# Strassen–Winograd chains of the ConvFFN up-projection: the first sum's split and the second sum's transfer taken earlier in the split order

## The chip, the cores and the metric

The kernel runs on one core of a Trainium2 chip. The metric is the device time of one execution in microseconds (us), smaller is better.

## The reference, cut to what matters

The reference is a small causal decoder trunk in fp32: one attention layer and one recurrent (RG-LRU) layer on x of 512 tokens by 1024 features, each followed by a gated ConvFFN. What the change touches is the up-projection `x @ w_up` of the ConvFFN:

```python
D_MODEL = 1024
SEQ = 512
DEPTH = 2
D_FF = 3 * D_MODEL
FFN_CONV_WIDTH = 3
...
def conv_ffn(x, w_up, conv_w, conv_b, w_down):
    u = causal_dwconv(x @ w_up, conv_w, conv_b)
    g, v = u[..., :D_FF], u[..., D_FF:]
    return (jax.nn.gelu(g, approximate=True) * v) @ w_down
...
    for layer in range(DEPTH):
        ...
        x = x + rms_norm(h, norm_mix_post[layer])
        h = rms_norm(x, norm_ffn_pre[layer])
        h = conv_ffn(h, ffn_w_up[layer], ffn_conv_w[layer], ffn_conv_b[layer], ffn_w_down[layer])
        x = x + rms_norm(h, norm_ffn_post[layer])
```

`w_up` is 1024 by 6144 in each of the two layers.

## The kernel before, in words

**Splitting.** Every fp32 operand of a matmul is split into two tiles, hi (ScalarE, ACT, copies the block to the matmul's format, L211) and lo (VectorE, DVE, subtracts hi from the block, L212). A product is then three matmuls: hi·hi, hi·lo and lo·hi. One split of a 128x512 block is one ACT and one DVE instruction.

**Chunks and chains.** The up-projection of a layer is cut into 24 chunks of 256 output features, each 1 MB of weights, loaded by SyncE (SP, `load`, L408) into a `raw` tile of four blocks of 128x512. There are three `raw` buffers. Of the 24 chunks, 20 a layer (`SEVEN`: ten indices, two halves each) go through `seven`. There a chunk is a *chain*: a Strassen–Winograd step that makes the 2x2 block product with seven products of 128 features, 512 inputs and 256 tokens instead of eight. Layer 0's chains take the trace from about 530 to 790 us, layer 1's from about 1077 to 1330 us.

**The sums of weight blocks.** A chain needs sums of its four blocks. They are made in place. The blocks are called w11, w12, s1 (which arrives as A21) and a22:

- `ahead`: s1 += block a22, which gives the first sum S1. An accumulating DMA of 256 KB, issued by GpSimd (POOL, L248), which reads the block from memory again.
- `across`: s1 += block w11, the second sum S2. The same kind of DMA. It may start only when S1 has been split, since it overwrites it.
- `left`: w11 += block A21, which gives the third sum S3. The same kind of DMA, after w11 has been split.
- `lower`: w12 += s1 on DVE (L274), the fourth sum S4.

So a chain has seven splits, named by what they hold: w11, w12, s1, s2, s3, s4, a22. Product 1 reads w11, 2 reads w12, 3 reads s4, 4 reads a22, 5 reads s1, 6 reads s2 and 7 reads s3.

**What sets the order.** `stream` (L260) makes for all 20 chains of a layer one list of items (splits, and issues of transfers and adds). Each item has a position: ten per chain (`CYCLE`), plus an offset that is written down in a table. The list is sorted by position and only the resulting order counts. `pump` (L366) takes pieces off the head of the list when fewer than 14 of the split pairs are in use (`HALVES`). A split is then written to ACT's and DVE's program at that point. Each engine runs its instructions in program order, so a split that waits for a transfer holds up all that stands behind it on ACT and on DVE. A POOL issue likewise stands in POOL's program in the order of the list, and waits there for the split of the block that it overwrites.

**The other user of these engines.** TensorE (PE) runs the products in a fixed order with a few plain products filled in between (`quarters`, `rows`). Their results are taken out by ACT and DVE: `part<-ps` copies of products 1, 5 and 6 (ACT L1124), an add of `part` into the PSUM tile after product 3 (DVE L1128), another after product 7 (DVE L1133), the convolution's first tap (ACT L845) and other taps (DVE L849), GELU (ACT L867) and the gate's multiply (DVE L871). Product 4 of a chain accumulates onto what L1133 wrote, so PE waits for L1133 there. `L1115` is the matmul line of all chain products.

Of the kernel before, what the change touches and what calls it, by code (L numbers as in the profile page):

```python
# [125 lines left out]
def kernel(  # L126
# [112 lines left out]
    def blocks(i):  # L239

        raw = raws[i]
        return {
            n: raw[:, 4 * b : 4 * b + 4, :] for b, n in enumerate(("w11", "w12", "s1", "a22"))
        }

    def add_block(i, to, b):
        assert i < state["dma"]
        nc.gpsimd.dma_start(blocks(i)[to], plan[i][3][0][0][:, 4 * b : 4 * b + 4, :], accum_op=ALU.add)  # L248

    def ahead(i):  # L250
        add_block(i, "s1", 3)

    def free_slots(n):

        end = CYCLE * n
        free = [CYCLE * c + r for c in range(n) for r in ((6, 7, 9) if c < 2 or c > 13 else (6, 7))][2:] + [end, end + 1]
        assert not {CYCLE * c + a for c in range(n) for a in AT.values()} & set(free)
        return free

    def stream(i0, n):  # L260

        items = []
        for c in range(n):
            i, o = i0 + c, CYCLE * c

            def left(i=i):
                add_block(i, "w11", 2)

            def across(i=i):
                add_block(i, "s1", 0)  # L270

            def lower(i=i):
                x = blocks(i)
                nc.vector.tensor_tensor(x["w12"], x["w12"], x["s1"], op=ALU.add)  # L274

            if c:
                items.append((o - 7, (None, lambda i=i: ahead(i))))
            for at, item in (
                (-6, ("w11", "w11")), (-5.9, (None, left)), (0, ("s1", "s1")), (0.4, ("w12", "w12")),
                (1.5, (None, across)), (5, ("s2", "s1")), (5.1, (None, lower)), (7, ("s3", "w11")),  # L280
                (8.5, ("s4", "w12")), (10.6, ("a22", "a22")),
            ):
                if isinstance(item[0], str):
                    item = ((i, item[0]), lambda i=i, h=item[1]: [blocks(i)[h]], item[0] == "a22")
                items.append((o + at, item))
        free = free_slots(n)
        direct = up["direct"]
        at = 8
        for key, loads, cuts, length in direct:
            u = free[at]  # L290
            if loads:
                items.append((u - EARLY, (None, loads)))
            items.append((u - 1, ((i0, key), cuts, False)))
            at += length
        return [item for _, item in sorted(items, key=lambda x: x[0])]
# [42 lines left out]
    def refill():  # L338

        i = state["cv"]  # L340
        if i >= state["dma"]:
            return
        if plan[i][0] == "quad":
            pieces.extend(strided_stream(i))
            state["cv"] += 24
            return
        if plan[i][0] == "seven":
            n = 1
            while plan[i + n][0] == "seven":
                n += 1  # L350
            pieces.extend(stream(i, n))
            state["cv"] += n
        else:
            if plan[i + 1 : i + 2] and plan[i + 1][0] == "seven":
                pieces.append((None, lambda: ahead(i + 1)))
            parts = parts_of(plan[i][0], raws[i])
            pieces.extend(plain(i, j, r, j == len(parts) - 1) for j, r in enumerate(parts))
            state["cv"] += 1
# [1446 lines left out]
```

## Time and profile before

| what | value |
|---|---|
| median of 3 runs | 1431.22 us (1428.69 to 1431.68) |
| the profiled execution | 1429.75 us, of which the span 1427.9 us |
| granted TensorE clock, mean | 0.992 |
| PE busy | 97% of the span |
| DVE busy | 78% |
| ACT busy | 56% |
| POOL busy | 17% |

The span is what the profiler recorded, and 1.85 us lie around it. The table gives averages: whether an engine's wait costs time is read from the place where PE, busy for 97% of the span, stands still. In the timeline a row gives the start in us, the duration, engine, line, operation, tiles, the count of equal instructions in a row and in brackets the idle time of the engine before it with what ended it. A row of the windows gives a stretch of the span, then each engine's busy time in it (and instructions), the granted clock, the busy share of the DMA engines, and GB/s.

### The profile page before, as it was taken

To read this page: it belongs to the slowest core of one execution; us is meant where nothing else is said; L and a number is where in the kernel's file an instruction comes from. 1 tells how busy PE (TensorE), PEld (TensorE's weight loads), DVE (VectorE), ACT (ScalarE), POOL (GpSimd) and SP (SyncE) were. 2 spreads that over 40 slices of the span, in tenths; PEclk is the share of its full clock that TensorE was granted. 3 is DMA by queue.
4 is the path that set the end of the run, shared out by engine and by line. 5 is a ranking of instruction groups with operands and counts; after the bars stand their busy time and mean duration, and the time that the engine had idled before them with its cause. 6 is when DMAs were issued, how large, how long until landed. Compare 5 with 4: busy or idle time off the path is not lost.

```text
span 1427.9 us, 25674 instructions
## 1 busy us (share of the span) xinstructions
PE 1390.4 (97%) x9749; PEld 1287.5 (90%) x9749; DVE 1114.2 (78%) x2189; ACT 800.9 (56%) x1670; POOL 236.4 (17%) x392
## 2 busy tenths in 40 slices
PE   9999999999999989999999999999998999999998
PEld 7989989999998889899998888999898899998886
DVE  6576898887865997888877758779898888876853
ACT  7343465363635655666655545589456566654641
POOL 0341332131300111222210001000111122211000
PEclk9999999999999999999999999999999999999999
DMA  7553454564756446776663532322455777755411
GB/s 223 181 147 108 121 177 150 172 184 138 209 153 242 149 97 169 178 172 177 150 172 100 199 126 100 137 90 95 142 148 118 178 177 178 188 130 134 172 71 59
DMA packets 70643, 214.62 MB, mean 150 GB/s; under 512 B 10816, under 2 KB 14360, under 8 KB 58744
## 3 DMA queue, kind: packets, MB, share of 16 engines
q1 hardware_dynamic: 42552, 153.34, 31.3%
q0 software_dynamic: 27120, 58.60, 20.1%
q8 instruction: 76, 1.25, 0.4%
q10 hardware_dynamic: 848, 1.05, 0.2%
q14 instruction: 47, 0.39, 0.1%
HBM read 193.99 MB, written 18.96 MB: 149 GB/s over the span
## 4 chain that ended last, share of the span: by engine, by line
PE 36%; issue 35%; DMA 21%; DVE 4%; POOL 2%; ACT 1%; POOLq 0%; DVEq 0%; SPq 0%; ACTq 0%
DMA raw<-in_ffn_w_up_dram 18%; PE acc L477 11%; PE ps L1115 9%; PE v L1312 6%; PE ps L477 5%; POOL raw L248 2%; PE v L1250 1%; DVE wlo L212 1%; DMA ft<-turned 1%; PE S L1458 1%; PE O L1524 1%; DMA raw<-in_attn_w_qkv_dram 1%; ACT whi L211 1%; PE S L1406 1%; DMA turned<-T 1%
## 5 line engine op out<-in xcount | busy, mean ns | idle before, releaser
L212 DVE TENSOR_TENSOR wlo<-raw,whi 128x512 fp32r<-128x512 f32 x628 | 416.7, 686 | 144.8 <-ACT whi L211 144.4
L211 ACT ACTIVATE whi<-raw 128x512 fp32r<-128x512 f32 x628 | 373.1, 626 | 221.3 <-DMA raw<-in_ffn_w_up_dram 77.1
L1115 PE MATMUL ps<-T,whi 128*128 128x256 f32 x1344 | 242.1, 279 | 11.7 <-ACT part L1124 11.6
L477 PE MATMUL ps<-hT,whi 128*128 128x256 f32 x1376 | 238.1, 277 | 1.3 <-ACT whi L211 1.3
L1115 PE MATMUL ps<-hT,whi 128*128 128x256 f32 x1344 | 239.2, 278 | 0.0
L1115 PEld LDWEIGHTS ps<-T,whi 128*128 128x128 f32 x1344 | 207.7, 190 | 16.9 <-ACT part L1124 14.1
L477 PEld LDWEIGHTS ps<-hT,whi 128*128 128x128 f32 x1376 | 208.4, 188 | 2.2 <-ACT whi L211 1.5
L1115 PEld LDWEIGHTS ps<-hT,whi 128*128 128x128 f32 x1344 | 205.6, 189 | 1.4
L477 PE MATMUL ps<-hT,wlo 128*128 128x256 f32 x688 | 190.2, 276 | 0.4 <-DVE wlo L212 0.4
L1115 PE MATMUL ps<-T,wlo 128*128 128x256 f32 x672 | 186.9, 278 | 0.0
L1115 PE MATMUL ps<-hT,wlo 128*128 128x256 f32 x672 | 186.0, 277 | 0.0
L248 POOL DMA_DIRECT2D raw<-in_ffn_w_up_dram x120 | 104.4, 971 | 447.1 <-DVE wlo L212 429.5
L477 PE MATMUL acc<-whi,ahi 128*128 128x512 f32 x336 | 131.4, 391 | 0.0
L477 PE MATMUL acc<-whi,alo 128*128 128x512 f32 x336 | 131.0, 390 | 0.2
L477 PE MATMUL acc<-wlo,ahi 128*128 128x512 f32 x336 | 130.8, 389 | 0.0
L477 PEld LDWEIGHTS ps<-hT,wlo 128*128 128x128 f32 x688 | 129.4, 188 | 0.6 <-DVE wlo L212 0.6
L1115 PEld LDWEIGHTS ps<-T,wlo 128*128 128x128 f32 x672 | 127.4, 190 | 0.0
L1115 PEld LDWEIGHTS ps<-hT,wlo 128*128 128x128 f32 x672 | 127.2, 189 | 0.0
L1312 PE MATMUL v<-whi,hT 128*128 128x512 f32 x320 | 107.0, 397 | 0.0
L1115 PE MATMUL ps<-last,whi 128*128 128x256 f32 x448 | 84.8, 287 | 14.5 <-DVE ps L1133 13.3
L1124 ACT ACTIVATE part<-ps 128x256 f32<-128x256 f32 x168 | 63.1, 376 | 46.4 <-PE ps L1115 44.9
L849 DVE SCALAR_TENSOR_TENSOR u<-ps,cols,u 128x511 f32<-128x511 f32 x112 | 83.6, 746 | 4.3 <-ACT u L845 2.4
(223 smaller groups left out, 2488.7 us busy)
## 6 DMA issues: line engine op xcount, KB each, us to landing
raw<-in_ffn_w_up_dram SPq DMA_DIRECT2D x48, 1024.0 KB
raw<-in_attn_w_qkv_dram SPq DMA_DIRECT2D x34, 1024.0 KB
raw<-in_ffn_w_up_dram POOLq DMA_DIRECT2D x120, 256.0 KB, 5.9
raw<-in_ffn_w_down_dram SPq DMA_DIRECT2D x14, 1024.0 KB
dw<-in_ffn_w_down_dram SPq DMA_DIRECT2D x40, 256.0 KB
raw<-in_lru_w_in_dram SPq DMA_DIRECT2D x8, 1024.0 KB
turned<-T POOLq DMA_DIRECT2D x26, 256.0 KB, 2.6
ft<-turned POOLq DMA_DIRECT2D x104, 64.0 KB, 4.6
```

The costliest lines, as they stand in the source:

```text
L211: nc.scalar.activation(hi, raw, AF.Copy)
L212: nc.vector.tensor_tensor(lo, raw, hi.bitcast(F32), op=ALU.subtract)
L248: nc.gpsimd.dma_start(blocks(i)[to], plan[i][3][0][0][:, 4 * b : 4 * b + 4, :], accum_op=ALU.add)
L477: mm(dst, l[a], r[b], start=start and n == 0, stop=stop and n == 2)
L849: nc.vector.scalar_tensor_tensor(u[:, d:], ps[:, : S - d], wc, u[:, d:], op0=ALU.mult, op1=ALU.add)
L1115: mm(dst, W[wa][0][:, k, :], right[n](ha, k), start=n in (1, 5) and k == q == 0, stop=k == 3 and q == 2, skip_group_check=True,)
L1124: later(1, lambda: nc.scalar.activation(to, dst, AF.Copy))
L1250: mm(banks[t], hT[a][:, k, t * P : (t + 1) * P], W[b][k % 2][:, 0, :], start=u == n == 0, stop=u == 3 and n == 5,)
L1312: mm(bank, hT[a][:, k, t * P : (t + 1) * P], W[b][k % 2][:, 0, :], start=(k, a, b) == (0, 0, 0), stop=(k, a, b) == (KD - 1, 1, 0),)
L1406: mm(Sp[a // 2][:, o + lo : o + 256], q[hh][:, a * P : (a + 1) * P], k[hh][:, k0 : (a + 1) * P], start=True, stop=True)
L1458: mm(ps[:, c], q[hh][:, c], k[hh][:, c], start=True, stop=True)
L1524: mm(po[:, c], vtile(v, r, 2 * gi + hh), pts[gi][:, r], start=gi == 0, stop=gi == 1)
```

## The change

The table of offsets in `stream` gets other numbers for three of its items.

```diff
             if c:
-                items.append((o - 7, (None, lambda i=i: ahead(i))))
+                items.append((o - 11, (None, lambda i=i: ahead(i))))
             for at, item in (
-                (-6, ("w11", "w11")), (-5.9, (None, left)), (0, ("s1", "s1")), (0.4, ("w12", "w12")),
-                (1.5, (None, across)), (5, ("s2", "s1")), (5.1, (None, lower)), (7, ("s3", "w11")),
+                (-6, ("w11", "w11")), (-5.9, (None, left)), (-4.4, ("s1", "s1")), (-4.3, (None, across)),
+                (0.4, ("w12", "w12")), (5, ("s2", "s1")), (5.1, (None, lower)), (7, ("s3", "w11")),
                 (8.5, ("s4", "w12")), (10.6, ("a22", "a22")),
```

The split of s1 goes from 0 to -4.4, `across` from 1.5 to -4.3 and `ahead` from -7 to -11. One chain is ten positions, so at -4.4 the split of s1 of chain c+1 stands at 5.6 of chain c: behind the split of s2 of chain c (5) and ahead of its s3 (7) and s4 (8.5). Before, it stood at 10, behind both. PE's and SP's programs keep their order, and so does POOL's (per chain `ahead`, `left`, `across`). On ACT and DVE three splits change places in each chain: s3(c), s4(c), s1(c+1) become s1(c+1), s3(c), s4(c).

ACT, early in the 20 chains of layer 0. `raw1182` is chain 1, `raw1201` chain 2; `whi1248`, `whi1250` and `whi1253` are the three splits, `last` is a filled-in product's split, L845 the first tap for chain 0. Before:

```order
L1124 ACTIVATE part1245_6775<-ps1244_6762 128x256
L211 ACTIVATE whi1248_6795<-raw1182_6296 128x512
L867 ACTIVATE u1241_6755<-u1241_6755 128x512
L1124 ACTIVATE part1246_6776<-ps1247_6781 128x256
L211 ACTIVATE last1185_6325<-B1229_6651 128x512
L211 ACTIVATE whi1250_6827<-raw1182_6296 128x512
L845 ACTIVATE u1252_6843<-ps1225_6634,cols248_1410,neg1165_6173 128x512
L211 ACTIVATE whi1253_6845<-raw1201_6382 128x512
L1124 ACTIVATE part1245_6775<-ps1244_6762 128x256
```

The same nine places of ACT's program now:

```order
L1124 ACTIVATE part1245_6775<-ps1244_6762 128x256
L211 ACTIVATE whi1248_6795<-raw1201_6382 128x512
L867 ACTIVATE u1241_6755<-u1241_6755 128x512
L1124 ACTIVATE part1246_6776<-ps1247_6781 128x256
L211 ACTIVATE last1185_6325<-B1229_6652 128x512
L211 ACTIVATE whi1250_6828<-raw1182_6296 128x512
L845 ACTIVATE u1252_6844<-ps1225_6635,cols248_1410,neg1165_6173 128x512
L211 ACTIVATE whi1253_6846<-raw1182_6296 128x512
L1124 ACTIVATE part1245_6775<-ps1244_6762 128x256
```

`whi1248` is now s1 of chain 2, `whi1250` s3 of chain 1, and s4 of chain 1 (`whi1253`) stands behind L845, where s1 of chain 2 stood.

ACT, two chains later. `raw1237` is chain 3, `raw1259` chain 4. Before, the three splits at the top are s2, s3 and s4 of chain 3, and behind the tap of L845 come s1 and w12 of chain 4:

```order
L211 ACTIVATE whi1285_7061<-raw1237_6694 128x512
L211 ACTIVATE whi1287_7066<-raw1237_6694 128x512
L211 ACTIVATE whi1290_7084<-raw1237_6694 128x512
L845 ACTIVATE u1292_7101<-ps1273_6967,cols248_1410 128x512
L211 ACTIVATE whi1293_7103<-raw1259_6887 128x512
L211 ACTIVATE whi1296_7123<-raw1259_6887 128x512
```

The same six places now:

```order
L211 ACTIVATE whi1285_7061<-raw1237_6694 128x512
L211 ACTIVATE whi1287_7066<-raw1259_6887 128x512
L211 ACTIVATE whi1290_7085<-raw1237_6694 128x512
L845 ACTIVATE u1292_7102<-ps1273_6968,cols248_1410 128x512
L211 ACTIVATE whi1293_7104<-raw1237_6694 128x512
L211 ACTIVATE whi1296_7125<-raw1259_6887 128x512
```

s1 of chain 4 is now ahead of s3 and s4 of chain 3, and of the tap; s4 of chain 3 is behind the tap. DVE's L212 rows change places in the same way.

## The prediction

> **What bounds the kernel now.** First the page's busy times, then what PE waits for over the whole span, then the timeline of PE in the two stages of chains.
>
> ```profile
> PE 1390.4 (97%) x9749; PEld 1287.5 (90%) x9749; DVE 1114.2 (78%) x2189; ACT 800.9 (56%) x1670; POOL 236.4 (17%) x392
> ```
>
> PE bounds the kernel. A change that adds and removes no matmul can move the time only where PE stands still or runs below its clock. The view of waits, PE's two largest and then ACT's on the adding transfers:
>
> ```profile
> PE ps L1115 <- DVE ps L1133: 13.3, 12, 3.7
> PE ps L1115 <- ACT part L1124: 11.6, 4, 4.6
> ...
> ACT whi L211 <- DMA raw<-in_ffn_w_up_dram: 77.1, 41, 6.7
> ```
>
> ACT waits 77.1 us in 41 places for a transfer into `raw` (nearly once for each of 40 chains), but PE's waits in chains are only these two groups, 24.9 us together. In the middle of a stage nothing comes through to PE (columns: window, its length, PE, PEld, DVE, ACT, POOL busy with counts, clock, DMA share, GB/s):
>
> ```profile
> 640.00:680.00 40.00, 40.00 (x310) 38.21 (x309) 34.96 (x57) 26.81 (x50) 7.83 (x9) 1.00 0.73 189
> ```
>
> PE is busy for 40.00 of 40 us there, although ACT waits in each of these chains. So the gain is to be looked for only where PE is idle. The timeline of PE, rows with idle time in brackets:
>
> ```profile
> 573.58 0.80 PE L1115 MATMUL ps<-last,whi 128*128 128x256 f32 x2 [3.73 <-DVE ps L1133]
> ...
> 753.64 0.51 PE L1115 MATMUL ps<-last,whi 128*128 128x256 f32 x2 [0.39 <-DVE ps L1133]
> ...
> 768.66 0.50 PE L1115 MATMUL ps<-last,whi 128*128 128x256 f32 x2 [0.94 <-DVE ps L1133]
> ...
> 776.43 0.51 PE L1115 MATMUL ps<-T,whi 128*128 128x256 f32 x2 [0.64 <-ACT part L1124]
> ...
> 784.08 0.51 PE L1115 MATMUL ps<-last,whi 128*128 128x256 f32 x2 [0.47 <-DVE ps L1133]
> ...
> 1119.48 0.80 PE L1115 MATMUL ps<-last,whi 128*128 128x256 f32 x2 [3.20 <-DVE ps L1133]
> ...
> 1299.12 0.50 PE L1115 MATMUL ps<-last,whi 128*128 128x256 f32 x2 [0.38 <-DVE ps L1133]
> ...
> 1314.25 0.50 PE L1115 MATMUL ps<-last,whi 128*128 128x256 f32 x2 [0.99 <-DVE ps L1133]
> ...
> 1323.06 0.51 PE L1115 MATMUL ps<-T,whi 128*128 128x256 f32 x2 [1.66 <-ACT part L1124]
> ```
>
> Both layers show one picture: one long stall in front of product 4 of chain 2 (573.58 and 1119.48), and a tail of short ones at the stage's end. The remaining idle time in L1124's group, one wait of 4.6 us at each stage's start, stands ahead of any moved split and stays.
>
> **Why PE stalls at chain 2.** The timelines of POOL, SP, ACT and DVE ahead of 573.58, and the transfer as the chain of waits gives it:
>
> ```profile
> 559.26 1.75 POOL L248 DMA_DIRECT2D raw<-in_ffn_w_up_dram  x2 [5.96 <-DVE wlo L212]
> ```
>
> ```profile
> 559.79 9.90 DMA raw<-in_ffn_w_up_dram
> ```
>
> ```profile
> 560.79 0.33 SPq L408 DMA_DIRECT2D raw<-in_ffn_w_up_dram  x1
> ```
>
> ```profile
> 563.53 1.15 ACT L211 ACTIVATE whi<-raw 128x512 fp32r<-128x512 f32 x2 [2.78 <-DMA raw<-in_ffn_w_up_dram]
> ...
> 569.78 2.19 ACT L211 ACTIVATE whi<-raw 128x512 fp32r<-128x512 f32 x4 [2.26 <-DMA raw<-in_ffn_w_up_dram]
> ```
>
> ```profile
> 555.03 0.68 DVE L212 TENSOR_TENSOR wlo<-raw,whi 128x512 fp32r<-128x512 f32 x1
> ...
> 558.28 1.28 DVE L212 TENSOR_TENSOR wlo<-raw,whi 128x512 fp32r<-128x512 f32 x2
> ...
> 561.29 1.53 DVE L849 SCALAR_TENSOR_TENSOR u<-ps,neg,u 128x511 f32<-128x511 f32 x2
> ...
> 573.09 0.43 DVE L1133 TENSOR_TENSOR ps<-ps,part 128x256 f32<-128x256 f32 x1
> ```
>
> POOL's two issues at 559.26 are `across` of chain 3 and `ahead` of chain 4, back to back, both held until DVE has split s1 of chain 3 (the second of the pair at 558.28). `ahead` lands 9.90 us after 559.79. ACT gets to s2 of chain 3 at 563.53 and to s1 of chain 4 only at 569.78, having waited 2.78 and 2.26 us. DVE follows, and L1133, which product 4 of chain 2 needs, stands behind these splits and starts at 573.09.
>
> **The change part by part.** No instruction is added or removed and no queue is passed: POOL's rows and SP's loads keep their order. What moves is the time at which s1 is split, and with it `across` and the `ahead` that POOL issues behind it. s1 of chain 3 takes the place of s3 of chain 2, whose DVE row is at 555.03: 3.25 us earlier than the row at 558.28, and some 3.9 earlier than the second of that pair. `across` then goes at about 555.8 and `ahead` at 556.3. With the mid-stage landing of 5.50 us,
>
> ```profile
> 644.99 5.50 DMA raw<-in_ffn_w_up_dram
> ```
>
> `across` has landed at 561.3 and `ahead` at 561.8 to 562.5. ACT then stands for s2 of chain 3 at 561.3 instead of 563.53, and s1 of chain 4 follows without a wait. s3, s4, the tap, w12 run behind. On DVE, from the end of s2's hi (562.0), nine rows stand up to and with w12's lo (L274, L1128, L871, five lo and L849's pair): about 7.0 us from 0.69 for a 128x512 row (569.0), then L1133's 0.43: 569.5. PE wanted to start product 4 at 573.58 − 3.73 = 569.85. The stall goes with no margin left.
>
> - *Stalls at chain 2*: 3.73 + 3.20 = 6.93 us, less 0.5 a layer that I leave because of the margin: −5.9.
> - *The clock behind them.* The windows there:
>
> ```profile
> 570.00:575.00 5.00, 1.43 (x6) 1.43 (x7) 4.23 (x7) 2.87 (x6) 1.75 (x2) 0.82 0.41 70
> 575.00:580.00 5.00, 5.00 (x39) 5.00 (x38) 3.48 (x6) 4.25 (x9) 0.86 (x1) 0.84 0.84 236
> 580.00:585.00 5.00, 5.00 (x46) 5.00 (x45) 4.19 (x7) 3.53 (x7) 1.75 (x2) 1.00 0.52 136
> ...
> 1115.00:1120.00 5.00, 1.80 (x14) 1.60 (x13) 3.62 (x7) 3.09 (x6) 1.75 (x2) 0.93 0.39 81
> 1120.00:1125.00 5.00, 5.00 (x34) 5.00 (x33) 3.21 (x7) 3.35 (x7) 0.86 (x1) 0.72 0.84 197
> ```
>
> Full clock is 46 matmuls in 5 us, 9.2 a us. From 570 PE had 10 − 3.58 = 6.42 us, worth 59 matmuls, and ran 45: 14 lost, 1.5 us. In layer 1, 10 − 3.20 = 6.8 us, worth 62.6, ran 48: 1.6 us. Sum −3.1 if both stalls go. The Trainium skill, "TensorE: Matmul & The Clock Gate", section "What's actually happening", has the array at half rate after an idle window of about 3.4 us until about 3.4 us of work: as an estimate 1.7 us for each stall, 3.4 for two. The trace agrees in size (0.82 and 0.84, 0.93 and 0.72 granted), though 3.20 us of idle was enough here; by that rule the sum would be 0.3 us better.
> - *The tails*: 0.39 + 0.94 + 0.64 + 0.47 = 2.44 and 0.38 + 0.99 + 1.66 = 3.03. The cause is the same wait of ACT on s2, as this row of ACT ahead of 776.43 shows:
>
> ```profile
> 773.76 0.63 ACT L211 ACTIVATE whi<-raw 128x512 fp32r<-128x512 f32 x1 [5.63 <-DMA raw<-in_ffn_w_up_dram]
> ```
>
> With `across` issued half a chain earlier such a wait of 5.63 us goes; s1 of the next chain may wait at its new place for `ahead`, by up to the 2.26 seen above. I take the tails as gone: −5.5. Bounds: nothing gained, and all gained.
> - *A new stall at chain 1.* s4 of chain 1 stood ahead of L845 of chain 0, which waits for PE; now it stands behind it.
>
> ```profile
> 545.39 0.78 ACT L845 ACTIVATE u<-ps,cols,neg 128x512 f32<-128x512 f32 x1 [1.16 <-PE ps L1115]
> 546.07 0.62 ACT L211 ACTIVATE whi<-raw 128x512 fp32r<-128x512 f32 x1
> ```
>
> ```profile
> 546.73 0.69 DVE L212 TENSOR_TENSOR wlo<-raw,whi 128x512 fp32r<-128x512 f32 x1 [1.68 <-ACT whi L211]
> ```
>
> ```profile
> 546.57 0.39 PE L1115 MATMUL ps<-hT,whi 128*128 128x256 f32 x2
> 546.79 0.28 PE L1115 MATMUL ps<-hT,wlo 128*128 128x256 f32 x1
> ```
>
> The place behind L845 yields hi at 546.07 + 0.62 = 546.69 and lo at 546.73 + 0.69 = 547.42. PE's product 3 wants hi at 546.57 and lo at 546.79. It waits 0.12 for the one and then for the other, 0.65 to 0.85 us with the handovers; I take 0.75 a layer: +1.5. Bounds: 0, where PE is later there anyway, and the 1.16 us that ACT waits at the tap on top, 1.9 a layer. Behind the waiting tap now stand s4 and all ACT rows after it; further on PE has slack for it.
> - *Mid-stage*: PE is at 40.00 of 40, so ACT's shorter waits are worth nothing. s3 and s4 are later by one split (0.69 on DVE) and by s1's wait, where it has one; this is hidden as long as `ahead` lands in time.
>
> Sum: −5.9 − 3.1 − 5.5 + 1.5 = −13.0. On the profiled execution's own 1429.75 us that makes 1416.75. It lies 1.47 below the median of 1431.22, so against the median I say 1418.2.
>
> **What is late next.** PE comes to chain 4's product 4 some 4.7 us earlier (3.73 − 0.5 + 1.5). DVE has to draw that in:
>
> ```profile
> 565.00:570.00 5.00, 4.85 (x43) 4.65 (x42) 2.89 (x5) 1.64 (x3) 0.00 (x0) 1.00 0.96 279
> ...
> 585.00:590.00 5.00, 5.00 (x47) 5.00 (x46) 4.93 (x10) 3.22 (x8) 0.86 (x1) 1.00 0.96 240
> 590.00:595.00 5.00, 5.00 (x34) 4.50 (x33) 4.96 (x9) 2.01 (x5) 0.00 (x0) 1.00 0.68 182
> ```
>
> From 565 to 595 DVE is busy 2.89 + 4.23 + 3.48 + 4.19 + 4.93 + 4.96 = 24.68 of 30 us: 5.3 idle, enough by 0.6.
>
> **The rivals.**
>
> 1. *The transfer meets the load.* `ahead` of chain 4 still takes 9.90 us, since the 1 MB load at 560.79 runs into it: it lands at 566.3, 4 us late on my path, and ACT stands at s1 with s3 and s4 behind it, so the stall at chain 2 stays at about 3 us, with its clock loss. For it: the DMA engines are at 0.96 and 279 GB/s in 565 to 570. Against: an issue at 556.3 has 4.5 us before that load. The Trainium skill, "DMA: Bandwidth & Descriptors", section "Issuing engines are not separate DMA queues", has transfers of all issuers interleave on the same 16 engines; the trace agrees (9.90 us with a load beside it, 5.50 without one at its start), and no run here shows whether the earlier issue escapes it. Then only the tails' 5.5 less 1.5 stay: −4.0, 1427.2.
> 2. *DVE becomes the bound* in 565 to 600: it cannot draw in the 4.7 us, and up to that much comes back in each layer at chain 4 in place of chain 2: 13.0 − 9.4 = 3.6, so 1427.6.
> 3. *Slower: the loop of the s1 splits.* Split of s1(c), `across`, `ahead`(c+1), landing, split of s1(c+1) is a loop, and s3 and s4 now stand behind its end on ACT.
>
> ```profile
> 644.45 1.75 POOL L248 DMA_DIRECT2D raw<-in_ffn_w_up_dram  x2 [6.68 <-DVE wlo L212]
> ...
> 656.76 1.75 POOL L248 DMA_DIRECT2D raw<-in_ffn_w_up_dram  x2 [7.01 <-DVE wlo L212]
> ```
>
> The period is 12.31 us. The split itself takes 0.62 on ACT and 0.69 on DVE; with the rows among which it stands I allow 3 from its start to POOL's pair (an estimate), and the second issue is 0.5 on. With landings of 5.50 some 3.3 us of the period are spare. It decides where landings are above 8.8 chain after chain. At 9.90 each of some 36 chains would be 1.1 us longer: +40 us, 1471. Against: landings of the mid-stage are near 5.5.
> 4. *It does nothing.* The transfers go when their data are ready, and POOL's order is the same; if s1's new place is reached late, since `pump` gives it only when 14 split pairs allow, all waits move together: 1431.2, with up to 1.5 either way.
>
> **How the numbers follow.** A difference of under 0.2%, 2.9 us, can't be told from no change. Forecast 0.60 (1411 to 1423, by the bounds of the tails' and chain 1's terms). Rival 1 0.13, rival 2 0.06: both about 1427, 4 below the median, of which 0.16 count as faster and 0.03 as the same. Rival 4 0.12: 0.10 the same, 0.02 slower. Rival 3 0.09, slower. So faster 0.76, same 0.13, slower 0.11. The range, 1411 to 1429, takes in the forecast and rivals 1 and 2, and leaves out rivals 3 and 4.
>
> **What would show it.** Right: PE's rows in front of product 4 of chain 2 show under 1 us of idle in both layers, the clock there is 1.00, ACT's wait on transfers falls from 77.1 us to under 30, the pair on POOL starts by 557, a new idle of about 0.7 us stands in front of product 3 of chain 1. Wrong: idle time <-ACT or DVE in mid-stage PE rows, `ahead` landings near 9 us chain after chain, ACT rows at s1 with new waits of several us, or the same stalls at chain 2.

## The result, and the profile after

The changed kernel takes 1411.76 us (median of 4 runs, 1410.9 to 1412.89) against 1430.65 us for the kernel before beside it (4 runs, 1428.69 to 1431.68). The ratio is 0.987, 95% interval 0.9853 to 0.9887: 18.9 us less. The prediction had said 1418.2, a gain of 13.0 us, and a range of 1411 to 1429. Times here are medians; the ratios are worked out from the single runs, so that they can differ a little from the quotient of two medians.

The profiled execution of the changed kernel took 1412.89 us, with a span of 1411.1 us: 16.8 us less than the span before. First the view of waits, PE's groups (total, times, longest), then ACT's row for the adding transfers.

```profile
PE ps L1115 <- ACT part L1124: 9.3, 2, 4.6
PE ps L1115 <- DVE ps L1133: 3.5, 4, 2.1
...
PE ps L1115 <- DVE wlo L212: 0.5, 2, 0.2
```

```profile
ACT whi L211 <- DMA raw<-in_ffn_w_up_dram: 2.0, 4, 1.0
```

ACT waited 77.1 us in 41 places, now 2.0 in 4. Of PE's waits for L1124 only the two at the stages' starts are left. One of L1133's four lies in the chains (0.55 us, below). The others, at 188, 212 and 348 us, lie ahead of the chains, in the attention layer, whose list wasn't changed.

The place of the long stall, chain 2 of layer 0: timelines of POOL, SP, ACT and DVE.

```profile
555.55 1.75 POOL L248 DMA_DIRECT2D raw<-in_ffn_w_up_dram  x2 [2.71 <-DVE wlo L212]
```

```profile
560.89 0.33 SPq L408 DMA_DIRECT2D raw<-in_ffn_w_up_dram  x1
```

```profile
561.03 0.63 ACT L211 ACTIVATE whi<-raw 128x512 fp32r<-128x512 f32 x1
561.86 1.16 ACT L211 ACTIVATE whi<-raw 128x512 fp32r<-128x512 f32 x2 [0.20 <-DMA raw<-in_ffn_w_up_dram]
```

```profile
569.34 0.43 DVE L1133 TENSOR_TENSOR ps<-ps,part 128x256 f32<-128x256 f32 x1
```

`across` of chain 3 and `ahead` of chain 4 go at 555.55, not 559.26. ACT splits s2 of chain 3 at 561.03 without a wait, and s1 of chain 4 at 561.86 after 0.20 us. L1133 starts at 569.34, in time for PE, which now runs through (windows of both layers, then mid-stage):

```profile
565.00:570.00 5.00, 5.00 (x47) 5.00 (x46) 4.79 (x9) 3.77 (x7) 1.72 (x2) 1.00 0.95 192
570.00:575.00 5.00, 5.00 (x47) 5.00 (x46) 4.82 (x8) 4.45 (x9) 1.25 (x2) 1.00 0.86 254
...
1110.00:1115.00 5.00, 5.00 (x47) 5.00 (x46) 4.30 (x8) 4.45 (x9) 1.61 (x2) 1.00 0.87 270
1115.00:1120.00 5.00, 5.00 (x47) 5.00 (x46) 4.19 (x7) 3.91 (x7) 0.98 (x2) 1.00 0.77 130
640.00:680.00 40.00, 40.00 (x318) 38.51 (x317) 34.26 (x56) 26.53 (x50) 7.81 (x9) 1.00 0.71 169
```

PE has 47 matmuls in each 5 us, at a clock of 1.00, where the first layer had 6 in 570 to 575. In mid-stage it was full before and is full now.

Two stalls came in PE's timeline: in front of product 3 of chain 1 (in both layers; layer 0's is shown), and a small one in layer 1.

```profile
546.29 0.50 PE L1115 MATMUL ps<-hT,whi 128*128 128x256 f32 x2
547.02 0.38 PE L1115 MATMUL ps<-hT,wlo 128*128 128x256 f32 x1 [0.23 <-DVE wlo L212]
...
1134.47 0.50 PE L1115 MATMUL ps<-last,whi 128*128 128x256 f32 x2 [0.55 <-DVE ps L1133]
```

The small one is absent in the trace of the kernel with only the split's number moved (below), whose order is the same, so the order alone does not make it. (`last` in PE's rows holds the right side of product 4. The `last` row in the lists of the change is the split of that side, a sum of blocks of tokens, and not a filled-in product's, as was said there.)

Where the time went is best read from PE's starts, since PE runs the same matmuls in the same order in both. A chain has 84 matmuls of L1115; below are the starts of each 84th in us, before, after and their difference, worked out from the two traces. Rows that are left out keep the difference above them; `end` is the last of the 1680 starts of a layer.

```
layer 0   0    521.69   521.86    +0.16
          1    539.90   539.45    -0.45
          2    554.73   555.11    +0.38   stall at chain 1
          4    584.67   579.59    -5.08   stall at chain 2 gone
          6    609.95   604.54    -5.40
         17    750.37   744.20    -6.18   tail
         18    764.83   757.93    -6.90   tail
         19    780.73   771.66    -9.06   tail
        end    797.85   788.01    -9.85   tail
layer 1   0   1068.87  1060.64    -8.22
          1   1086.32  1078.60    -7.72
          2   1101.16  1094.25    -6.91   stall at chain 1
          4   1130.69  1118.73   -11.96   stall at chain 2 gone
          6   1155.84  1144.20   -11.64
         17   1295.85  1283.85   -12.00   tail
         18   1310.39  1297.58   -12.80   tail
         19   1327.37  1311.32   -16.05   tail
        end   1344.48  1327.66   -16.82   tail
```

From 6 to 16 of each layer nothing moves: mid-stage gave and cost nothing. From the end of layer 0 to the start of layer 1 the changed kernel's execution lost 1.6 us again, where nothing was moved: a dip of the clock, told in the last section.

### The profile page after: what moved, and what is told of

Same layout as the page of the kernel before. It is cut to its first block, busy times and chain, and to the rows that moved or that the text cites. A ratio compares the mean times of both kernels' runs of the same rounds, so it can differ in the third digit from the quotient of the medians.

```text
span 1411.1 us, 25652 instructions
## 1 busy us (share of the span) xinstructions
PE 1385.5 (98%) x9749; PEld 1285.1 (91%) x9749; DVE 1114.3 (79%) x2189; ACT 805.9 (57%) x1670; POOL 236.5 (17%) x392
## 4 chain that ended last, share of the span: by engine, by line
PE 82%; DVE 9%; ACT 6%; issue 1%; DMA 1%; POOL 0%; DVEq 0%; SPq 0%; ACTq 0%
PE ps L1115 35%; PE acc L477 24%; PE ps L477 9%; PE v L1312 7%; DVE wlo L212 3%; PE v L1250 1%; DVE xb L1616 1%; ACT whi L211 1%; DVE u L849 1%; PE O L1524 1%; PE S L1458 1%; DMA raw<-in_attn_w_qkv_dram 1%; ACT sig L1637 1%; PE ps L1092 1%; PE ps L1094 1%
## 5 line engine op out<-in xcount | busy, mean ns | idle before, releaser
L212 DVE TENSOR_TENSOR wlo<-raw,whi 128x512 fp32r<-128x512 f32 x628 | 417.6, 686 | 109.2 <-ACT whi L211 108.8
L1115 PE MATMUL ps<-T,whi 128*128 128x256 f32 x1344 | 240.9, 278 | 9.3 <-ACT part L1124 9.3
L1115 PE MATMUL ps<-hT,whi 128*128 128x256 f32 x1344 | 239.3, 278 | 0.0
L1115 PEld LDWEIGHTS ps<-T,whi 128*128 128x128 f32 x1344 | 207.5, 189 | 12.8 <-ACT part L1124 9.7
L1115 PEld LDWEIGHTS ps<-hT,whi 128*128 128x128 f32 x1344 | 205.3, 189 | 1.9 <-ACT whi L211 0.4
L1115 PE MATMUL ps<-T,wlo 128*128 128x256 f32 x672 | 186.7, 278 | 0.0
L1115 PE MATMUL ps<-hT,wlo 128*128 128x256 f32 x672 | 186.3, 277 | 0.5 <-DVE wlo L212 0.5
L248 POOL DMA_DIRECT2D raw<-in_ffn_w_up_dram x120 | 104.1, 938 | 418.5 <-DVE wlo L212 370.5
L1115 PEld LDWEIGHTS ps<-hT,wlo 128*128 128x128 f32 x672 | 127.0, 189 | 1.0 <-DVE wlo L212 1.0
L1115 PEld LDWEIGHTS ps<-T,wlo 128*128 128x128 f32 x672 | 127.1, 189 | 0.0
L1124 ACT ACTIVATE part<-ps 128x256 f32<-128x256 f32 x168 | 63.7, 379 | 88.8 <-PE ps L1115 86.7
L1115 PE MATMUL ps<-last,whi 128*128 128x256 f32 x448 | 81.1, 279 | 4.9 <-DVE ps L1133 3.5
```

The source lines that it names most:

```text
L212: nc.vector.tensor_tensor(lo, raw, hi.bitcast(F32), op=ALU.subtract)
L1115: mm(dst, W[wa][0][:, k, :], right[n](ha, k), start=n in (1, 5) and k == q == 0, stop=k == 3 and q == 2, skip_group_check=True,)
L1124: later(1, lambda: nc.scalar.activation(to, dst, AF.Copy))
```

## The experiments

Theory A is the prediction's: the split of s1, its transfer and the next chain's first sum's transfer were late, ACT and DVE were held at s2 and s1, and PE lost time only at chain 2 and in the tails. The rivals are a common delay (B), POOL's order alone (C), s2's wait alone (D), and a kernel that does not care in mid-stage. All times are medians beside runs of the kernel before on the same chip.

**Only the first chains, only the last chains.** The old numbers for the other chains:

```diff
+            early = c <= 5
...
-                items.append((o - 11, (None, lambda i=i: ahead(i))))
+                items.append((o - 7, (None, lambda i=i: ahead(i))))
...
-(-4.4, ("s1", "s1")), (-4.3, (None, across)),
+(-4.4 if early else 0, ("s1", "s1")), (-4.3 if early else 1.5, (None, across)),
```

and `early = c >= 12` for the second kernel. `ahead` is at its old position for all chains, which changes no order (next experiment).

> The changed order only for the first chains of a layer (c up to 5), the old order for the rest. Theory A (the late splits of s1 hold up PE at separate places, and each place pays by itself): the long stalls at chain 2 and their clock loss go, worth 5.5 + 5.1 us by the starts of PE's matmuls in the two traces, the new stall at chain 1 costs 0.8 a layer, the tails stay. So 10.6 - 1.6 = 9.0 below the kernel before: about 1421.6 (1419.5 to 1424), no PE idle above 1 us at chain 2, and the tail's rows as before. Theory B (one common delay: what is gained early is needed again at the tail): the tail gets worse or better by more than 1 us against the kernel before, and the time is outside 1419.5 to 1424.

> The changed order only for the last eight chains of a layer (c from 12), the old order for the rest. Theory A (each place pays by itself): the tails' 3.7 + 4.4 us by the starts of PE's matmuls go, the stalls at chain 2 (3.7 and 3.2 us) stay: about 8.1 below the kernel before, 1422.5 (1420.5 to 1425). Together with the run of the first chains the two gains should add up to the whole change's within 2.5 us. Theory B (one common delay): the tail's gain depends on the early chains, so this run gains under 4 us or over 12.

Measured: 1420.39 us for the first chains, ratio 0.9942 (0.9926 to 0.9959), and 1420.97 us for the last, 0.994 (0.9925 to 0.9955), against 1430.32 us. PE's rows of the first kernel at the tails, then of the second at chain 2:

```profile
762.85 0.51 PE L1116 MATMUL ps<-last,whi 128*128 128x256 f32 x2 [0.84 <-DVE ps L1134]
...
1314.46 0.50 PE L1116 MATMUL ps<-T,whi 128*128 128x256 f32 x2 [1.53 <-ACT part L1125]
```

```profile
574.65 0.54 PE L1116 MATMUL ps<-last,whi 128*128 128x256 f32 x2 [3.19 <-DVE ps L1134]
...
1118.89 0.79 PE L1116 MATMUL ps<-last,whi 128*128 128x256 f32 x2 [4.11 <-DVE ps L1134]
```

Each kernel keeps the stalls that its old half had (0.84 for 0.94, 1.53 for 1.66, and 3.19 and 4.11 for 3.73 and 3.20). By PE's starts the first wins 5.46 and 5.05 us at chain 2, as the whole change does, and the second 4.45 and 5.18 in the tails, as the whole change does. By the medians the gains are 9.9 and 9.4 us, together 19.3 where the whole change has 18.9; each is known to some 2 us. Theory B falls.

**One number of the three.** The transfers' positions back at the old ones, only the split moved:

```diff
-                items.append((o - 11, (None, lambda i=i: ahead(i))))
+                items.append((o - 7, (None, lambda i=i: ahead(i))))
...
-(-4.4, ("s1", "s1")), (-4.3, (None, across)),
+(-4.4, ("s1", "s1")), (1.5, (None, across)),
```

> Of the change's three numbers only the one of s1's split (0 to -4.4); the two transfers keep their old positions, 1.5 and -7. Theory A: a transfer on POOL goes when its data are ready, in the order of the list, and these two positions change neither; every engine has the changed kernel's order, so this is the whole change: 1410 to 1414, equal to the changed kernel within 2 us. Rival: the transfers' own positions matter, then it lies more than 3 us off.

Measured: 1410.48 us, ratio 0.987 (0.985 to 0.9889), the change itself. In the sorted list the issues on POOL follow each other in the same order with `ahead` at -7 or -11 and `across` at 1.5 or -4.3. The split's number is the whole change.

**The second sum's transfer left out of the old order.** Product 6 then reads the first sum in place of the second, so this kernel computes something else.

```diff
-                (1.5, (None, across)), (5, ("s2", "s1")), (5.1, (None, lower)), (7, ("s3", "w11")),
+                (5, ("s2", "s1")), (5.1, (None, lower)), (7, ("s3", "w11")),
```

> The kernel before, its old order, with the second sum's transfer left out (s2 then splits the first sum again, so product 6 and what follows use another block): what that transfer costs at most in the old order. Theory A (the stalls at chain 2 and in the tails come from s2's wait for this transfer and from the first sum's transfer queued behind it): both go, 14 to 20 us below the kernel before: 1410 to 1416. Rival (DVE's load sets them): the stalls at chain 2 stay above 1.5 us, less than 8 us gained.

Measured: 1409.38 us, ratio 0.9855 (0.9842 to 0.9869), 0.6 below the range that theory A gave. PE's waits:

```profile
PE ps L1115 <- ACT part L1124: 9.3, 2, 4.6
PE ps L1115 <- DVE ps L1133: 2.4, 3, 1.5
```

By PE's starts it wins 5.3 and 4.9 us at chain 2 and 4.4 and 5.2 in the tails, to 0.2 us what the change wins there, without moving a split. So the stalls came from this transfer's landing and from the other transfer's place behind it, together; DVE's splits and adds, the same here, did not set them. It has no stall at chain 1, where the order is the old one.

**The first sum's transfer ahead of the second's on POOL.** In the old order, one number:

```diff
-                items.append((o - 7, (None, lambda i=i: ahead(i))))
+                items.append((o - 9, (None, lambda i=i: ahead(i))))
```

> The kernel before with one number other: the adding transfer of the first sum of chain c+1 is issued on POOL ahead of the second sum's transfer of chain c, not behind it; all splits keep their old order. Theory A (both waits count: s2 for the second sum's transfer, s1 for the first sum's): only s1's wait of 2.26 us ahead of the stall at chain 2 goes, the stall shrinks from 3.7 to 1 to 2 us and its clock loss goes, the tails stay since ACT waits at s2 there: 4 to 9 us below the kernel before, about 1424 (1421 to 1427). Theory C (only the first sum's transfer counts, since it stands behind the other one on POOL): the whole gain comes without moving a split, 1410 to 1414. Theory D (only s2's wait counts): within 2 us of the kernel before.

and the changed kernel with `across` back at 1.5 behind `ahead` at -11:

```diff
-(-4.4, ("s1", "s1")), (-4.3, (None, across)),
+(-4.4, ("s1", "s1")), (1.5, (None, across)),
```

> The changed kernel, but with the second sum's transfer back at its old position 1.5, which puts the next chain's first sum's transfer ahead of it on POOL; all splits stand as in the changed kernel. Theory A: PE has hardly any wait left there that a transfer sets, so the time is that of the changed kernel, 1410 to 1414; s2 may wait up to 0.5 us longer, hidden in mid-stage. Rival (s2's transfer is now the tight one, as it goes 0.5 us later and meets the other one on the DMA engines): PE idle at chain 2 or in the tail comes back, 2 to 6 us above the changed kernel.

Measured: 1435.03 us, ratio 1.0044 (1.0031 to 1.0057), slower than the kernel before and outside all three theories; and 1416.78 us, 0.9909 (0.9895 to 0.9923), 5.0 above the changed kernel, where theory A had expected none and its rival 2 to 6. PE's, POOL's and ACT's timelines of the first of the two:

```profile
570.42 0.51 PE L1115 MATMUL ps<-last,whi 128*128 128x256 f32 x2 [1.47 <-DVE ps L1133]
576.15 0.50 PE L1115 MATMUL ps<-hT,whi 128*128 128x256 f32 x2 [2.70 <-ACT part L1124]
...
1126.93 0.80 PE L1115 MATMUL ps<-hT,whi 128*128 128x256 f32 x2 [4.98 <-ACT part L1124]
```

```profile
568.34 1.75 POOL L248 DMA_DIRECT2D raw<-in_ffn_w_up_dram  x2 [6.72 <-DMA raw<-in_ffn_w_up_dram]
```

```profile
575.20 0.63 ACT L211 ACTIVATE whi<-raw 128x512 fp32r<-128x512 f32 x1 [4.78 <-DMA raw<-in_ffn_w_up_dram]
```

The stall at chain 2 shrinks to 1.47 as theory A had it. But `ahead` of chain 5 needs its 1 MB load, and POOL stands 6.72 us waiting for it, with `across` of chain 4 behind it. s2 of chain 4 then waits 4.78 us on ACT, the `part` copy behind it is late, and PE stands 2.70 and 4.98 us one chain on. The second kernel shows the same chain of waits (POOL, ACT, PE):

```profile
567.79 1.75 POOL L248 DMA_DIRECT2D raw<-in_ffn_w_up_dram  x2 [4.83 <-DMA raw<-in_ffn_w_up_dram]
```

```profile
573.83 0.63 ACT L211 ACTIVATE whi<-raw 128x512 fp32r<-128x512 f32 x1 [3.62 <-DMA raw<-in_ffn_w_up_dram]
```

```profile
574.78 0.38 PE L1115 MATMUL ps<-hT,whi 128*128 128x256 f32 x1 [1.49 <-ACT part L1124]
```

By PE's starts it loses 4.9 us against the changed kernel in chains 2 to 5 of the two layers, and nothing in the tails. The old POOL order, `across` first, is the better one here since its data are there first. Theories C and D fall too: in the first kernel a part of the stall went with `ahead` alone, and not all of it.

**A longer loop.** `ahead` moved behind `left` on POOL, the rest as changed:

```diff
-                items.append((o - 11, (None, lambda i=i: ahead(i))))
+                items.append((o - 4.5, (None, lambda i=i: ahead(i))))
```

> The changed kernel with the first sum's transfer issued behind the third sum's of the same chain, not ahead of it: everything else as in the changed kernel. That lengthens on purpose the loop of the slower rival (split of s1, transfer, split of the next s1): the third sum's transfer is issued 7 us after the place where the first sum's stands now. Theory A: mid-stage has only some 3 us to spare in that loop, so s1 waits on ACT in nearly each chain with s3 and s4 behind it, PE gets idle in mid-stage, and the time is at least 10 us above the changed kernel: 1425 to 1500. Rival (the transfers are hidden in mid-stage anyway): within 3 us of the changed kernel.

Measured: 1610.7 us, ratio 1.1266 (1.1243 to 1.129): slower than the whole range of either theory. ACT's and POOL's timelines in mid-stage:

```profile
647.67 0.63 ACT L211 ACTIVATE whi<-raw 128x512 fp32r<-128x512 f32 x1 [6.39 <-DMA raw<-in_ffn_w_up_dram]
...
665.57 0.63 ACT L211 ACTIVATE whi<-raw 128x512 fp32r<-128x512 f32 x1 [6.79 <-DMA raw<-in_ffn_w_up_dram]
```

```profile
639.61 1.75 POOL L248 DMA_DIRECT2D raw<-in_ffn_w_up_dram  x2 [6.44 <-DVE wlo L212]
...
657.01 1.75 POOL L248 DMA_DIRECT2D raw<-in_ffn_w_up_dram  x2 [6.83 <-DVE wlo L212]
```

A chain takes 657.01 − 639.61 = 17.4 us, not 12.31. The pair on POOL is now `left` and `ahead`, held until w11 has been split, and s1 is among the next splits behind w11. So s1 waits 6 to 7 us in each of the chains shown, and DVE and ACT do what stands behind only afterwards. This loop runs through the split of w11 and not, as in the prediction's slower rival, through `across`. It shows what it costs when ACT meets a landing at s1 in each chain, but not that the rival's own loop can bind. In the changed kernel `ahead` goes right behind `across`, and no such wait is left.

**The split half as far, without its transfer.** This kernel had s1's split at -2.5, but left `across` at -4.3, ahead of it:

```diff
-(-4.4, ("s1", "s1")), (-4.3, (None, across)),
+(-2.5, ("s1", "s1")), (-4.3, (None, across)),
```

Its expectation speaks of a kernel in which the pair is moved, which this one isn't. Here s1's split reads the second sum in place of the first (another computation), and waits for both transfers one after the other.

> The split of s1 and the second sum's transfer only half as far: s1 of chain c+1 between s3 and s4 of chain c. Theory A (a margin at chain 2 of one or two us, set by when the two transfers land): they go some 0.7 to 1.2 us later than in the changed kernel, L1133 for chain 2 is at most 0.5 us late, the tails stay gone, the stall at chain 1 stays: 1410 to 1415. Rival (the margin is nil, as the prediction had it): a stall of 0.7 to 1.2 us and a clock loss at chain 2 in each layer, 2 to 5 us above the changed kernel.

Measured: 1550.12 us, ratio 1.0841 (1.0822 to 1.086). It tells nothing on the margin, only once more what s1's wait costs: ACT's and PE's waits.

```profile
ACT whi L211 <- DMA raw<-in_ffn_w_up_dram: 204.0, 38, 10.1
```

```profile
PE ps L1115 <- DVE ps L1133: 79.6, 32, 7.3
```

**Half as far, and one step further.** The pair at -2.5 and -2.4 (s1 between s3 and s4 of the chain before), and at -5.2 and -5.1 (ahead of its s2):

```diff
-(-4.4, ("s1", "s1")), (-4.3, (None, across)),
+(-2.5, ("s1", "s1")), (-2.4, (None, across)),
```

> The split of s1 and the second sum's transfer behind it moved only half as far: s1 of chain c+1 stands between s3 and s4 of chain c. Theory A (a margin at chain 2 of 0.5 us or less, by the 569.34 at which L1133 starts in the changed kernel against the 569.85 at which PE had wanted it): s1 of chain 3 is split 0.7 to 1.2 us later than in the changed kernel, so a stall of 0 to 0.7 us a layer comes at chain 2, the stall at chain 1 stays, the tails stay gone: 1411 to 1415. Rival (only the whole way helps, since what counts is the place ahead of s3): the stalls at chain 2 stay above 2 us and the time above 1418.

> One step further than the change: s1 of chain c+1 is split ahead of s2 of chain c too. Theory A (the changed kernel has taken all that there is; s2 is now one split later and waits on ACT behind the first sum's transfer where that is late, at the stage's start and tail): 1410 to 1416, nothing gained. Rival (the earlier the better): 2 us or more below the changed kernel.

Measured: 1415.48 us, ratio 0.9898 (0.9885 to 0.9912), and 1418.88 us, 0.9923 (0.9909 to 0.9936), against 1410.5 to 1411.8 of the changed order. Both lie above what theory A gave, by 0.5 and 2.9 us. PE's rows of the first, then of the second:

```profile
573.75 0.50 PE L1115 MATMUL ps<-hT,whi 128*128 128x256 f32 x2 [0.52 <-ACT part L1124]
585.28 0.51 PE L1115 MATMUL ps<-last,whi 128*128 128x256 f32 x2 [1.69 <-DVE ps L1133]
```

```profile
533.33 0.80 PE L1115 MATMUL ps<-T,whi 128*128 128x256 f32 x2 [5.86 <-ACT part L1124]
...
598.67 0.50 PE L1115 MATMUL ps<-last,whi 128*128 128x256 f32 x2 [0.71 <-DVE ps L1133]
```

Half as far does not bring the long stall back at chain 2, but shorter ones come one and two chains on, 3.9 us by PE's starts in the two layers: the early chains have hardly any margin. One step further shows 1.2 us more at each stage's start (5.86 where 4.64 was) and small stalls of up to 0.83 as well. The place behind s2 is the best of the four that were run.

**The stall at chain 1.** Two ways to take it away: s1 of chain 2 at its old place, and s4 of chain 1 ahead of its s3.

```diff
+            early = c != 2
...
-(8.5, ("s4", "w12")), (10.6, ("a22", "a22")),
+(6.5 if c == 1 else 8.5, ("s4", "w12")), (10.6, ("a22", "a22")),
```

> The changed kernel, but s1 of chain 2 at its old place, so that s4 of chain 1 stands ahead of the tap again. Theory A (the stall at chain 1 is s4 behind the waiting tap, 0.8 us a layer by the starts of PE's matmuls): 1.6 below the changed kernel, about 1410, no idle in front of product 3 of chain 1. Rival (the early chains need the early split of chain 2's s1 too): the first sum's transfer of chain 3 goes later, ACT waits 1 to 2 us at s1 of chain 3, and a stall of up to 1.5 us a layer comes at chain 1 or 2: 1411 to 1415.

> The changed kernel, but s4 and s3 of chain 1 change places, so that s4, which product 3 needs first, stands ahead of the waiting tap and s3, which product 7 needs later, behind it. Theory A: the idle in front of product 3 of chain 1 goes, 0.8 us a layer by the starts of PE's matmuls, and nothing comes in its place: 1.6 below the changed kernel, 1408 to 1411. Rival (another row then holds PE there, or s3 is late for product 7): no gain, 1410 to 1414.

Measured: 1416.95 us, ratio 0.9909 (0.9894 to 0.9925), and 1410.88 us, 0.9866 (0.9852 to 0.9879). By PE's starts both win 0.8 us a layer at chain 1, so the stall is s4 behind the waiting tap. The first then pays at chain 3, where ACT's timeline shows a new wait at s1:

```profile
557.28 0.63 ACT L211 ACTIVATE whi<-raw 128x512 fp32r<-128x512 f32 x1 [2.41 <-DMA raw<-in_ffn_w_up_dram]
```

So the rival's mechanism came, and the time lies above the rival's range. By the starts it costs 3.9 us in the two layers, 2.3 more than is won. The kernel's median lies 5.2 to 6.5 above the changed order; 2.9 us of that stand in the profile ahead of the first chain, in the attention layer, where nothing was moved, and stay unexplained. The second has no stall in the chains left but those at the stages' starts (4.6 us, and two of 0.3, in each layer). The 1.6 us that it wins are less than the runs' spread: it can't be told from the changed kernel (1411.76 and 1410.48).

## Why the prediction was right, point by point

*What bounds, and where the gain is.* Right. Mid-stage moved by nothing, and the two kernels with half the change show that chain 2 and the tails pay separately. The gain itself came out too small: 13.0 us was said, and 18.9 came.

*The transfers' times.* Right: 555.55 for 555.8, ACT at s2 at 561.03 for 561.3, at s1 at 561.86 for 561.8 to 562.5, L1133 from 569.34 for 569.0. Rival 1 did not come: the load was issued at 560.89, and the earlier `ahead`, issued at 556.09, landed at 561.84, 5.75 us later. The view of L248, before and after (time from issue to landing, minimum, median, maximum):

```profile
DMA to landing us min/median/max: 4.1/5.9/10.3
```

```profile
DMA to landing us min/median/max: 4.1/5.5/8.5
```

The longest landing got shorter. The Trainium skill, "DMA: Bandwidth & Descriptors", section "Issuing engines are not separate DMA queues", has all issuers share the same 16 engines. That fits the 9.90 us before. Here the issue 4.8 us ahead of the load took 5.75 us.

*Sizes* (profiled executions, by PE's starts):

| term | predicted | measured |
|---|---|---|
| stalls at chain 2 with the clock behind | −5.9 − 3.1 = −9.0 | −5.46 − 5.05 = −10.5 |
| tails, up to the end of the chains | −5.5 | −4.45 − 5.18 = −9.6 |
| new stall at chain 1 | +1.5 | +0.83 + 0.81 = +1.6 |
| dip of the clock between the stages, in this execution | 0 | +1.6 |
| chain 4, starts of the stages | 0 | +0.1 |
| sum | −13.0 | −16.8 |

Two terms were too small. The 0.5 us a layer kept back at chain 2 was not needed, which is 1.0 of the 1.5 that are missing there. The tails were mis-sized. The sum left out one row of the kernel before, the last of layer 1's tail:

```profile
1330.72 0.50 PE L1115 MATMUL ps<-last,whi 128*128 128x256 f32 x2 [0.47 <-DVE ps L1133]
```

More than that, the idle time in brackets was taken for the cost. Two neighbouring starts of PE before, in the tail:

```profile
752.98 0.28 PE L1115 MATMUL ps<-hT,wlo 128*128 128x256 f32 x1
753.64 0.51 PE L1115 MATMUL ps<-last,whi 128*128 128x256 f32 x2 [0.39 <-DVE ps L1133]
```

The starts are 0.66 us apart, and 0.11 to 0.12 is usual in that stretch: 0.55 lost, with 0.39 in the bracket. The rest, 0.16 us in each wait, is hidden behind the end of the row ahead, which the profile models. The next start (753.86) is late by 0.11 us more. And some waits are too short for a row with a bracket: those at 738.78 and 746.07 cost 0.31 and 0.41 us. The same holds at chain 1: 0.23 in the bracket, 0.83 lost. There the estimate came out right because it was made from the times at which PE wanted its data, and not from a bracket.

The last 2 us, from 16.8 to 18.9, are the executions' spread: before's profiled one lies 0.9 below its median, after's 1.1 above its own. The dip of the clock, 1.6 us, is in the one profile and not in the other.

*The range.* Its low end was partly luck. The bounds that the prediction names, all of the tails (which the forecast already counts) and nothing lost at chain 1, lead from 1418.2 to 1416.7. Nothing in its working leads to 1411, and the measured 1411.76 lies 0.8 us inside.

*Rivals 2, 3 and 4.* DVE drew the 4.7 us in: no stall at chain 4 of layer 0, 0.55 in layer 1. The loop of the s1 splits was not reached, in this or any other run. Rival 4 did not come: the transfers went 3.7 us earlier, at 555.55. The change did what was predicted, though one of its three numbers does all of it.

## What to carry to other kernels

In an in-order queue, look not at who waits most (77 us on ACT), but at the few places where the bounding engine stands still, and ask which row there was queued behind a transfer; then move the start of that transfer, which may be the split or read that must come before it, and not the transfer's own position. Put issues on one queue in the order in which their data become ready, since one that waits for a load holds up the ready one behind it. Size a stall by the distance of neighbouring starts less the usual distance, not by the idle time in the row.

## What was not expected of the hardware

The clock did not dip in the same places in two executions. Between the two stages of chains, where the two programs are the same, PE was idle for 1.67 us in a 5 us window in both; first before, then after:

```profile
885.00:890.00 5.00, 3.33 (x27) 2.89 (x26) 4.91 (x9) 4.20 (x8) 0.00 (x0) 1.00 0.39 114
890.00:895.00 5.00, 5.00 (x47) 5.00 (x46) 1.57 (x3) 0.78 (x1) 0.00 (x0) 1.00 0.80 302
```

```profile
875.00:880.00 5.00, 3.33 (x25) 2.89 (x24) 4.92 (x10) 4.20 (x8) 0.00 (x0) 0.96 0.37 113
880.00:885.00 5.00, 5.00 (x33) 5.00 (x33) 1.19 (x2) 0.00 (x0) 0.00 (x0) 0.70 0.83 306
```

After it the clock was 0.70 and 14 matmuls of 47 were lost, 1.5 us; in the kernel before it stayed at 1.00. The order is not the reason, since the kernel with only the split's number moved has the changed kernel's order and shows no dip there:

```profile
875.00:880.00 5.00, 3.33 (x27) 3.12 (x27) 4.90 (x9) 3.82 (x8) 0.00 (x0) 1.00 0.31 107
880.00:885.00 5.00, 5.00 (x46) 5.00 (x46) 1.53 (x3) 0.78 (x1) 0.00 (x0) 1.00 0.65 243
```

The Trainium skill, "TensorE: Matmul & The Clock Gate", section "What's actually happening", has a free-running window of about 3.4 us. That fits a dip that comes in one execution and not in the next. That 1.67 us of idle in 5 us can be enough is the measurement's. What one execution loses by its clock can therefore differ by some 1.5 us, about what the medians of two kernels with one order differ by (1411.76 and 1410.48).
